# The 64x64 inverses of a delta-rule stage: products of both halves on two quarters of the tensor engine instead of one product with a diagonal left operand

## The chip, the cores and the metric

The kernel runs on one core of one Trainium2 chip. The metric is the time of one execution on the device, in microseconds: before the change 4966.08 us as the median of three runs (4948.15 to 4974.35). A core has five engines that matter here: TensorE (PE in the profile; its weight loads are PEld), VectorE (DVE), ScalarE (ACT), GpSimd (POOL) and SyncE (SP), which issues the DMAs.

## The reference, cut to what matters

The reference is a network of two blocks. Block 1 (a chunked mLSTM with dilated attention and a feed-forward part, two layers) and the attention, the merge and the experts of block 2 are not touched. The change lies in the second branch of block 2, a delta rule over 256 context tokens and then 512 tokens, in both directions, for 16 heads of 64 channels:

```python
def wkv_scan(s0, scan_in):
    def step(s, inp):
        w, kk, a, k, v, r = inp
        sa = jnp.einsum('dbhij,dbhj->dbhi', s, kk)
        s = s * w[..., None, :] - sa[..., :, None] * (kk * a)[..., None, :] + v[..., :, None] * k[..., None, :]
        return s, jnp.einsum('dbhij,dbhj->dbhi', s, r)
    return lax.scan(step, s0, scan_in)
```

A token's `sa` depends on all tokens before it. The kernel takes chunks of 64 tokens; within a chunk the dependence is a triangular system, so each chunk of each head and direction needs the inverse of a 64x64 triangular matrix.

## The kernel before

`rwkv` (L1499) works through eight blocks of 128 channels (two heads). A block has three groups of four chunks (four of context, then four and four of the 512 tokens), so there are 24 groups. The loop over `s` at the end of `rwkv` makes one pass for each group, and `weave` puts the steps of several generators side by side over `TT` = 36 ticks: `chain` of group s (the state over its four chunks), `newton` of group s + 1 once for each direction, `values` of group s + 1, `decays` and `products` of group s + 2, and as filler the projections of the next block (`mm` tiles in the profile, weights `wbh`, `wbl`). TensorE's instructions keep the order in which they are written (`pe = Pinned(...)`); the order on VectorE, ScalarE and GpSimd is set by the scheduler and by priorities (`high_priority`).

`newton` (L1723) takes the products G of a group, makes NB, and lays it out in fp16: N16 (L1733, ScalarE) and the rest NL (L1737, GpSimd). NB holds eight units of 64x64, four in partitions 0 to 63 and four in 64 to 127. Then `inverse` (L1957) runs 18 steps: `turned` is a transpose by 64x64 products with the unit matrix (two of it in each call), `prod` is one or two 64x64 products for each unit (15 of the steps), and each step ends in an evacuation to fp16 by ScalarE (`act`, L1986, tiles Yi and Zi) or VectorE (`plus`, L2000, tiles Ai and the first Yi). The last step adds into U (`keep`, L1745), which `chain` takes.

`prod` makes one instruction of 128x128 shape for two units, one in either half: its left operand (the stationary one) is a tile with the two units in diagonal blocks and zeros around them, its right operand has them stacked. So what is to stand on the left is copied into such a tile by `lay` (L1994, VectorE), half by half: Ly, Lv and Lz for each direction. N16 and NL are laid out in this way when they are made. All these tiles are cleared once by GpSimd (L1926).

Names in the rows: `n` is the PSUM bank of a step; `n<-Zi,Lv` is a product with moving operand Zi and left operand Lv; `c` the bank of the chain (`Xs`, `S`, `VS`, `KB`, `G`, `U`, `KR` its operands), `x` a bank of decays, products and transposes, `mm` one of the projections; `N` is N16 or N8; `id` and `tables` are unit matrices and masks.

Of the kernel before, what the change touches and what calls it, by code (L numbers as in the profile page):

```python
# [12 lines left out]
F16 = mybir.dt.float16  # L13
# [3 lines left out]
ALU = mybir.AluOpType  # L17
# [13 lines left out]
HL = 50  # L31
# [23 lines left out]
class Pinned:  # L55
    """An engine with its instructions in the order they are written in."""
# [9 lines left out]
class Core:  # L66
    """All engines so."""
# [7 lines left out]
class Feed:  # L75
    """Weights in the order of their use, 512 columns a tile, loaded ahead and split into two parts that one pass each carries."""

    def __init__(self, net, raw, split):
        self.net, self.nraw, self.nsplit = net, raw, split
        self.src, self.raws, self.tiles, self.over = [], [], {}, set()  # L80
        self.taken = self.dead = 0
        # another pool for what is loaded before weight number last
        self.more, self.last = None, 0

    def add(self, w, r0, c0, n, order=None, both=False):
        """1024 rows of n columns; returns the number of row tiles in a tile."""
        kt = min(KD, T // n)
        for rows in order or [range(k, k + kt) for k in range(0, KD, kt)]:
            self.src.append((w, r0 + rows[0] * P, rows[1] - rows[0], kt, c0, n, both))
        return kt  # L90
# [39 lines left out]
def part(gen, n):  # L130
    """The next n steps of a generator."""
# [11 lines left out]
def among(a, b, n):  # L143
    """A generator with n steps of another one after each of its own."""
# [5 lines left out]
def weave(ticks, *work):  # L150
    """Steps of several generators in turn: (generator or (function, its argument), from, to, number of steps)."""
# [12 lines left out]
def tables():  # L164
    """Constants of shapes alone, [128, n] each: for all of the program, for block 1, for block 2."""
# [20 lines left out]
    # axial rotation, token major: [128, token tile, 64]  # L186
# [23 lines left out]
class Net:  # L210
# [34 lines left out]
    def row(self, ap, n, pool=None, tag=None):  # L245
        """A DRAM row of n on all partitions."""
# [4 lines left out]
    def wtile(self, w, r0, c0, n):  # L251
        """128 rows of a weight, split into two parts that one pass each carries."""
# [16 lines left out]
    def rstd(self, out, ss, n, eps=1e-6, nc=None):  # L269
        """out = (ss / n + eps) ** -0.5"""  # L270
# [12 lines left out]
    def defer(self, n, f, *x):  # L283
        """f, n steps of the projections later."""
# [12 lines left out]
    def unit_t(self, w, c0, x, evac, n=P, tok=slice(0, T)):  # L297
        """Eight steps to a block of columns of a product, transposed: evac(psum [n, tokens])."""
# [19 lines left out]
    def unit_n(self, w, r0, c0, x, evac, pairs=(0, 1), order=((0, 1), (2, 3), (4, 5), (6, 7))):  # L318
        """Eight steps to 256 columns of a product of each pair of token tiles: evac(pair, psum [tokens, 2, 256])."""
# [23 lines left out]
    def norm_pair(self, p, g, x, pool, s=1):  # L343
        """Two token tiles of X, normed, to columns of the transposed operand: staged, s steps for each stage."""
# [36 lines left out]
    def layer(self, l, S):  # L381
        """The layers of block 1 in two parts: the order of what meets the weights; the work. The heads run on a plan of
        ticks, 24 for a head of the first kind (M) and 12 for one of the second (B), and projections are woven in."""
# [13 lines left out]
        # ---- what follows the projections  # L397
# [49 lines left out]
        def rope(nm, b):  # L447
            """Rotated queries or keys of two heads, split as the products of scores take them."""
# [57 lines left out]
        # ---- the order of the weights  # L506
# [34 lines left out]
        # ---- the heads  # L541
# [5 lines left out]
        def pofs(d, i, t):  # L547
            """Column of key tile i, query tile t among the kept blocks."""
# [89 lines left out]
        def turned(n, src, k):  # L638
            """128 columns of a mixed output, transposed and split."""
# [67 lines left out]
        # ---- the work  # L707
# [69 lines left out]
    def norms(self, name, g, S):  # L777
        """What the staged norm of the two pairs of token tiles takes, and a new transposed operand."""
# [5 lines left out]
    def block1(self):  # L784
        tc, nc, a = self.tc, self.nc, self.a
        with ExitStack() as st:
            # on the way into block 2: the transposed operand, and until then X
# [8 lines left out]
            # the table of functions, before data is there  # L796
# [30 lines left out]
    def final_part(self, p, s, k):  # L827
        """X times the final gain, 256 columns of a pair of token tiles, and their sums of squares before and after."""
# [11 lines left out]
    def final_rest(self, p, xs, mod, bank, x, s, n0):  # L840
        """X = rms_norm(X, final_g) of two token tiles; normed once more, scaled and shifted per feature, to columns of
        the transposed operand. Staged, s steps for each stage."""
# [52 lines left out]
    def gates(self, l, ps, q, tl):  # L895
        """The gates of block 1 from their sums: staged."""
# [85 lines left out]
    def ahead(self, S):  # L982
        """What block 2 takes from its conditions and its context alone."""
# [16 lines left out]
    def block2_params(self, pool):  # L1000
# [16 lines left out]
        # lambda, the same on all partitions  # L1017
# [11 lines left out]
    def attn_params(self, cp):  # L1029
        nc, a = self.nc, self.a  # L1030
        self.load_tables(2, cp)
        # gains of q and k folded into the rotation
# [24 lines left out]
    def mods(self, pool):  # L1057
        """Modulation vectors: per feature columns, and rows for the two that gate a residual."""
# [48 lines left out]
    def modulated_xt(self, tiles, s1, sh, xh, xl, pool, bank, back=None, first=0, to=None):  # L1107
        """Normalised token tiles -> split transposed operand, scaled and shifted per feature, or as it is to DRAM."""
# [21 lines left out]
    def normed_of(self, src, pool, out=None):  # L1130
        """src / rms, in a tile of the pool or over src."""
# [10 lines left out]
    def block2(self):  # L1142
# [17 lines left out]
        # the operands of the projections again as places for others: of [128, T], high and low  # L1160
# [26 lines left out]
    def attention(self):  # L1187
        """Differential attention, a quarter (two heads) at a time; while the heads of one quarter run, the
        projections of the next are woven in. Yields once before x is needed, with the function that gives
        banks, and once before the last quarter, whose fill it is sent."""  # L1190
# [5 lines left out]
        with ExitStack() as left:  # L1196
# [8 lines left out]
            def loads():  # L1205
                """256 columns of the weight at a time, split in two: four tiles of two row tiles each."""
# [26 lines left out]
            def bank_of(i, xh, xl, b, evac, last=False):  # L1233
                """Projection i of two token tiles to 256 columns."""
# [14 lines left out]
            def headed(nm, q, o, rotate, last):  # L1249
                """Queries or keys of two token tiles: normed by heads, rotated, and split as the products take them."""  # L1250
# [52 lines left out]
            def ahead(u):  # L1303
                """What a quarter takes from the context: keys and values."""
# [37 lines left out]
            def scores(n):  # L1342
                """Products of queries and keys, and their exponentials: 4 ticks for each of a unit's four maps."""
# [28 lines left out]
            def turned(u):  # L1372
                """A quarter's outputs, transposed."""
# [16 lines left out]
            def outs(n, x):  # L1390
                """The difference of a unit's maps, transposed, and its product with the values."""
# [91 lines left out]
    def wblock(self):  # L1483
        """The next two row tiles of a block of 128 columns, of weights laid [128, block, 8, 128], split in two; others are asked for ahead."""
# [14 lines left out]
    def rwkv(self, hxh, hxl, hch, hcl, mmt2, bank2, lead):  # L1499
        """Delta-rule heads by chunks of 64 tokens, a block of 128 channels (two heads) at a time, both  # L1500
        directions together and in three groups: 4 chunks of context, then 4 and 4 of x. While the chain
        over the chunks of one group runs, the inverses of the next, the decays of the one after it and
        the projections of the next block are woven in."""
# [7 lines left out]
        with ExitStack() as st:  # L1511
# [12 lines left out]
            # what no chain takes: gives way to the work that fills the last ones  # L1524
# [21 lines left out]
            def proj(b, dst, both=True):  # L1546
                """Shifted channels of block b, of context and x."""
# [1114 lines left out]
```

## Time and profile before

| what | us |
|---|---|
| median of three runs | 4966.08 |
| lowest, highest | 4948.15, 4974.35 |
| profiled execution, first to last instruction (span) | 4986.3 |
| TensorE busy in the span | 4530.2 |
| VectorE busy | 3463.8 |
| GpSimd busy | 2156.0 |
| ScalarE busy | 1993.8 |
| the stage with the 24 groups, 2030 to 3200 | 1170 |

Of the profiled execution the span is what is given; no other time of it is. Busy time of TensorE counts a product from its start to a modelled end, and products overlap: one that starts 0.03 us after another is still booked with its full 0.19 us. How fast a row of products goes is therefore read from start to start. The profile also gives the clock that TensorE was granted, as a share of full speed; it has two levels, 2.4 GHz (1.00) and 1.2 GHz (0.50).

### The profile page before, as it was taken

Reading aid. Unit: us, or ns where it says so; the run is one execution under the profiler, and the core shown is the slowest. Engines: PE = TensorE matmul, PEld = TensorE weight load, DVE = VectorE, ACT = ScalarE, POOL = GpSimd, SP = SyncE. Lnnn points to the kernel's source line nnn. Section 1 sums busy time; section 2 is a strip of 40 time slices with the busy share of each in tenths; the row PEclk is TensorE's granted clock in tenths of the full one; section 3 lists DMA queues with packets and bytes.
Section 4 is the critical chain, followed back from the end, with each engine's and each line's share of the span. In section 5 each row is a group of like instructions: output and inputs, shape, how many; then the busy total and the mean of one; then the engine's idle time right before and its main releaser. Section 6 shows DMA issues by size and latency. Waiting matters only on the chain. (4 is left out here: it accounts for less than half of the span.)

```text
span 4986.3 us, 78323 instructions
## 1 busy us (share of the span) xinstructions
PE 4530.2 (91%) x29167; PEld 3864.4 (78%) x29167; DVE 3463.8 (69%) x6705; ACT 1993.8 (40%) x4288; POOL 2156.0 (43%) x1715
## 2 busy tenths in 40 slices
PE   8999999999998998888898889889799889988987
PEld 6789897888888886677776767768677678877776
DVE  4654234655656654677777877668753989999999
ACT  3444334443325554344444444433222444333333
POOL 3324443324434332322232333144433247888886
PEclk8999999999999999788788888999678999999999
DMA  4234333235653211000000001462344447887886
GB/s 128 72 86 133 96 115 98 69 89 157 189 186 112 55 46 42 19 21 18 20 21 23 23 26 36 134 213 92 104 125 153 158 160 274 294 289 278 289 291 230
DMA packets 435687, 618.46 MB, mean 124 GB/s; under 512 B 32596, under 2 KB 318436, under 8 KB 435176
## 3 DMA queue, kind: packets, MB, share of 16 engines
q1 hardware_dynamic: 392104, 469.87, 30.0%
q0 software_dynamic: 36864, 134.23, 7.8%
q10 hardware_dynamic: 6336, 9.35, 0.6%
q8 instruction: 229, 3.75, 0.3%
q14 instruction: 154, 1.26, 0.1%
HBM read 549.36 MB, written 48.24 MB: 120 GB/s over the span
## 5 line engine op out<-in xcount | busy, mean ns | idle before, releaser
L63 POOL TENSOR_TENSOR wlo<-wraw,whi 128x512 fp32r<-128x512 f32 x451 | 614.9, 1369 | 897.3 <-ACT whi L63 850.6
L63 ACT CAST whi<-wraw 128x512 fp32r<-128x512 f32 x572 | 347.3, 617 | 564.4 <-PE mm L63 369.8
L63 PE MATMUL acc<-v,ah 128*128 128x512 f32 x1536 | 444.7, 414 | 4.3 <-ACT ah L63 4.3
L1495 POOL TENSOR_TENSOR wbl<-wblk,wbh 128x256 fp32r<-128x256 f32 (+1 forms) x184 | 148.3, 806 | 615.4 <-ACT wbh L1494 362.9
L63 PE MATMUL u<-hph,u 128*128 128x384 f32 x1504 | 400.6, 338 | 4.5 <-ACT x L63 4.5
L63 PE MATMUL mm<-whi,u 128*128 128x256 f32 x2048 | 377.2, 285 | 4.5 <-ACT u L63 2.7
L63 PE MATMUL acc<-v,al 128*128 128x512 f32 x768 | 264.2, 427 | 113.1 <-DVE al L63 112.8
L63 PEld LDWEIGHTS acc<-v,ah 128*128 128x128 f32 x1536 | 309.0, 202 | 68.0 <-ACT ah L63 4.6
L63 PE MATMUL mm<-xh,whi 128*128 128x512 f32 (+2 forms) x880 | 342.8, 390 | 8.0 <-ACT r L63 4.6
L63 PE MATMUL mm<-xh,wlo 128*128 128x512 f32 (+2 forms) x880 | 328.9, 374 | 0.0
L63 PEld LDWEIGHTS mm<-whi,u 128*128 128x128 f32 x2048 | 323.4, 193 | 6.5 <-ACT u L63 3.3
L63 PE MATMUL mm<-xl,whi 128*128 128x512 f32 (+2 forms) x880 | 328.4, 373 | 0.0
L63 POOL TENSOR_TENSOR u<-raw,u 128x1024 fp32r<-128x1024 f32 x94 | 273.3, 2908 | 81.0 <-ACT u L63 80.8
L63 ACT ACTIVATE gq<-gq 128x384 f32<-128x384 f32 x128 | 67.1, 524 | 595.4 <-DVE gq L63 595.4
L63 PE MATMUL mm<-wlo,u 128*128 128x256 f32 x1024 | 291.6, 285 | 5.0 <-POOL wlo L63 4.6
L63 PEld LDWEIGHTS acc<-v,al 128*128 128x128 f32 x768 | 151.5, 205 | 169.4 <-DVE al L63 140.4
L63 PEld LDWEIGHTS u<-hph,u 128*128 128x128 f32 x1504 | 275.4, 189 | 9.1 <-ACT x L63 4.9
L63 DVE SCALAR_TENSOR_TENSOR x<-gq,x 128x384 f32<-128x384 f32 x128 | 264.6, 2067 | 12.9 <-ACT gq L63 12.2
L63 POOL TENSOR_TENSOR v<-raw,v 128x1024 fp32r<-128x1024 f32 x64 | 195.1, 3048 | 171.7 <-ACT v L63 159.6
L63 PE MATMUL u<-hpl,u 128*128 128x384 f32 x752 | 253.5, 337 | 0.0
L63 PE MATMUL mm<-whi,xh 128*128 128x256 f32 x768 | 236.0, 307 | 0.0
L63 PE MATMUL mm<-whi,xl 128*128 128x256 f32 x768 | 219.5, 286 | 0.1
(608 smaller groups left out, 13232.8 us busy)
## 6 DMA issues: line engine op xcount, KB each, us to landing
raw<-in_ut_dram SPq DMA_DIRECT2D x128, 512.0 KB
raw<-in_peer_v_dram SPq DMA_DIRECT2D x128, 512.0 KB
wraw<-in_w_in_dram SPq DMA_DIRECT2D x184, 256.0 KB
wraw<-in_w_down_dram SPq DMA_DIRECT2D x160, 256.0 KB
wraw<-in_w_up_dram SPq DMA_DIRECT2D x152, 256.0 KB
mraw<-in_w_mod_dram SPq DMA_DIRECT2D x96, 256.0 KB
wg<-stage SPq DMA_DIRECT2D x12, 2048.0 KB
W<-wg SPq DMA_DIRECT2D x32, 768.0 KB
```

Of the source, the lines that this page charges most:

```text
L63: return lambda *a, **k: self.tc.keep_in_program_order(f(*a, **k))
L1495: (nc.vector if self.wn > WN and n % 2 else nc.gpsimd).tensor_tensor(lo, raw, hi.bitcast(F32), op=ALU.subtract)
```

## The change

The left operands are no longer laid out in diagonal blocks. `prod` makes two products of 64x64 shape for each pair of units instead of one of 128x128: the upper half of the partitions with the upper half of the result, the lower with the lower, each with its stacked operand as it was evacuated. With that `lay` and its copies go, the tiles Ly, Lv and Lz go, N16 and NL are stacked like NB and are each made by one instruction instead of two, and only U is cleared. The steps, their order and their evacuations stay. (The diff also drops comments and doc strings throughout the file, which moves line numbers by one to fourteen.)

```diff
-                for hf in H:
-                    nc.scalar.copy(N16[hf, u, hf], NB[hf])
+                nc.scalar.copy(N16[:, u], NB)
...
-                for hf in H:
-                    nc.gpsimd.tensor_tensor(NL[hf, u, hf], NB[hf], N16[hf, u, hf], op=ALU.subtract)
+                nc.gpsimd.tensor_tensor(NL[:, u], NB, N16[:, u], op=ALU.subtract)
...
-            N16, NL = (rest[0].tile([P, 8, P], F16, name=nm) for nm in ("N16", "NL"))
-            L_ = [[rest[0].tile([P, 4, P], F16, name=f"L{nm}{d}") for nm in "yvz"] for d in range(2)]
+            N16, NL = (rest[0].tile([P, 8, 64], F16, name=nm) for nm in ("N16", "NL"))
             U_ = rest[0].tile([P, 4, 2, P], F32, name="U")
-            for x in (N16, NL, *L_[0], *L_[1], U_):
-                nc.gpsimd.memset(x, 0.0)
+            nc.gpsimd.memset(U_, 0.0)
...
                 for n, (l, r) in enumerate(pairs):
-                    pe.matmul(ps[:, i * 64:(i + 1) * 64], l[:, i], r[:, i], start=n == 0, stop=n == len(pairs) - 1)
+                    for hf in H:
+                        pe.matmul(ps[hf, i * 64:(i + 1) * 64], l[hf, i], r[hf, i], start=n == 0, stop=n == len(pairs) - 1)
...
-        def act(ps, tag, left=None):
+        def act(ps, tag):
             t = t16(tag)
             with self.tc.high_priority(HP):
                 nc.scalar.copy(t, ps)
-            lay(left, t)
             return t
 
-        def lay(left, t):
-            if left is not None:
-                with self.tc.high_priority(HL):
-                    for hf in H:
-                        nc.vector.tensor_copy(left[hf, :, hf], t[hf])
...
-        Y = plus(turned(N8), 2.0, "Yi", Ly)
+        Y = plus(turned(N8), 2.0, "Yi")
         yield
-        plus(prod((Ly, N8)), 2.0, "Ai", Lv)
+        V = plus(prod((Y, N8)), 2.0, "Ai")
         yield
-        Y = act(prod((Lv, Y)), "Yi", Ly)
+        Y = act(prod((V, Y)), "Yi")
...
         for it in range(3):
-            A = plus(prod((N16, Y)), 2.0, "Ai", Lv if it < 2 else None)
+            A = plus(prod((N16, Y)), 2.0, "Ai")
             yield
-            Y = act(prod((Lz, A)), "Yi")
+            Y = act(prod((Z, A)), "Yi")
             yield
-            Z = act(prod((Lv, Z)), "Zi", Lz) if it < 2 else act(turned(Y), "Zi")
+            Z = act(prod((A, Z)) if it < 2 else turned(Y), "Zi")
             yield
-        plus(prod((N16, Y), (NL, Y)), 1.0, "Ai", Lv)
+        A = plus(prod((N16, Y), (NL, Y)), 1.0, "Ai")
         yield
-        keep(prod((Lv, Z)), Z)
+        keep(prod((A, Z)), Z)
```

How the change moves instructions is seen at two places. The first is TensorE early in the stage, at the third step of an inverse (Y = V Y); before, the left operand of the first direction is Lv_20448 and that of the second Lv_20451:

```order
L63 MATMUL mm_20489<-xl_15441,wbh_20522 128x512
L63 LDWEIGHTS Lv_20448
L63 MATMUL n_3909_20685<-Yi_3898_20633,Lv_20448 128x64
...
L63 LDWEIGHTS Lv_20451
L63 MATMUL n_3911_20694<-Yi_3900_20646,Lv_20451 128x64
...
L63 MATMUL mm_20489<-xh_15440,wbl_20523 128x512
```

and in the changed kernel:

```order
L62 MATMUL mm_20475<-xl_15441,wbh_20508 128x512
L62 LDWEIGHTS Ai_3903_20646
L62 MATMUL n_3909_20667<-Yi_3898_20615,Ai_3903_20646 64x64
...
L62 LDWEIGHTS Ai_3905_20657
L62 MATMUL n_3911_20678<-Yi_3900_20626,Ai_3905_20657 64x64
...
L62 MATMUL mm_20475<-xh_15440,wbl_20509 128x512
```

The left operand is now the evacuated tile itself, and each direction has eight pairs of load and product where it had four; the projections around them stay where they were, as do all other products of TensorE.

The second place is VectorE at the first two steps of an inverse in a later group, before:

```order
L1792 COPY VS_21628<-c_20443 64x128
L2000 SCALAR_TENSOR_TENSOR Yi_4147_21788<-tables_19359,n_4146_21779 128x256
L2000 SCALAR_TENSOR_TENSOR Yi_4149_21801<-tables_19359,n_4148_21792 128x256
L1994 COPY Ly_20447<-Yi_4147_21788 64x4x64 x2
L1994 COPY Ly_20450<-Yi_4149_21801 64x4x64 x2
L1804 SCALAR_TENSOR_TENSOR S_21818<-c_20443,WC_20594,Sw_21729 128x128 x2
L2000 SCALAR_TENSOR_TENSOR Ai_4153_21826<-tables_19359,n_4152_21821 128x256
L2000 SCALAR_TENSOR_TENSOR Ai_4155_21835<-tables_19359,n_4154_21830 128x256
L1994 COPY Lv_20448<-Ai_4153_21826 64x4x64 x2
L1994 COPY Lv_20451<-Ai_4155_21835 64x4x64 x2
L1671 SCALAR_TENSOR_TENSOR ta_21734<-ta_21734,kkn_20795 128x256
L1775 COPY Xs_21851<-c_20443 64x128
```

and in the changed kernel:

```order
L1987 SCALAR_TENSOR_TENSOR Yi_4147_21938<-tables_19359,n_4146_21929 128x256
L1789 COPY VS_21762<-c_20443 64x128
L1987 SCALAR_TENSOR_TENSOR Yi_4149_21949<-tables_19359,n_4148_21940 128x256
L1801 SCALAR_TENSOR_TENSOR S_21964<-c_20443,WC_20580,Sw_21883 128x128 x2
L1987 SCALAR_TENSOR_TENSOR Ai_4153_21976<-tables_19359,n_4152_21967 128x256
L1987 SCALAR_TENSOR_TENSOR Ai_4155_21987<-tables_19359,n_4154_21978 128x256
L1670 SCALAR_TENSOR_TENSOR ta_21888<-ta_21888,kkn_20797 128x256 x2
L1772 COPY Xs_22001<-c_20443 64x128
```

The copies into Ly and Lv are gone; the rest moves by a place or two.

## Rows read from the trace of the kernel before

**Rows 1.** The page: TensorE's granted clock in 40 slices of the span, tenths.
```profile
PEclk8999999999999999788788888999678999999999
```

**Rows 2.** Stage: length, busy PE, PEld, DVE, ACT, POOL (instructions), granted clock, DMA share, GB/s.
```profile
2030.00:3200.00 1170.00, 1026.14 (x9313) 824.09 (x9311) 894.74 (x2523) 506.68 (x1420) 343.29 (x517) 0.83 0.10 31
```

**Rows 3.** Groups of instructions, 2030 to 3200: busy us, mean ns | idle before, releasers.
```profile
L1994 DVE COPY Lv<-Ai 64x256 f16<-64x256 f16 x480 | 165.1, 344 | 6.8
...
L1994 DVE COPY Lz<-Zi 64x256 f16<-64x256 f16 x288 | 71.4, 248 | 10.9 <-ACT Zi L1986 6.1
L63 PE MATMUL c<-Xs,U 128*128 128x64 f32 x368 | 64.9, 309 | 28.0 <-DVE Y L1782 22.2 <-ACT Y L1780 3.3 <-DVE U L1745 1.1
...
L1994 DVE COPY Ly<-Yi 64x256 f16<-64x256 f16 x192 | 63.8, 332 | 3.0
...
L63 PE MATMUL n<-Zi,Lv 128*128 128x64 f16 x576 | 36.1, 203 | 47.3 <-DVE Lv L1994 47.3
...
L63 PE MATMUL n<-N,Ly 128*128 128x64 f16 x384 | 30.3, 222 | 20.4 <-DVE Ly L1994 19.2 <-ACT wbh L1494 0.4
...
L63 PE MATMUL n<-Yi,Lv 128*128 128x64 f16 x384 | 24.9, 209 | 14.2 <-DVE Lv L1994 14.0 <-ACT Zi L1986 0.2
```

**Rows 4.** Who waited for whom, 2030 to 3200: us in total, times, longest.
```profile
PE n L63 <- DVE Lv L1994: 61.3, 61, 2.0
...
PE n L63 <- DVE Ly L1994: 19.2, 34, 1.8
```

**Rows 5.** One wait in order of time: start us, us, engine, instruction, [idle before].
```profile
2407.86 0.74 DVE L2000 SCALAR_TENSOR_TENSOR Ai<-tables,n 128x256 f16<-128x256 f32 x2
...
2408.52 1.79 DVE L1994 COPY Lv<-Ai 64x256 f16<-64x256 f16 x4
...
2409.40 0.29 PE L63 MATMUL n<-Zi,Lv 128*128 128x64 f16 x4 [1.73 <-DVE Lv L1994]
...
2410.37 0.39 PE L63 MATMUL n<-Zi,Lv 128*128 128x64 f16 x4 [0.68 <-DVE Lv L1994]
```

**Rows 6.** Short stretches ahead of and behind falls of the clock, columns as in rows 2.
```profile
2406.50:2409.90 3.40, 1.46 (x11) 0.85 (x10) 3.32 (x7) 1.86 (x5) 3.17 (x5) 1.00 0.14 41
2409.90:2430.40 20.50, 20.03 (x113) 17.76 (x113) 9.37 (x28) 6.02 (x16) 4.53 (x5) 0.50 0.03 7
2034.40:2037.80 3.40, 1.41 (x16) 0.79 (x16) 3.26 (x9) 1.77 (x5) 2.10 (x3) 1.00 0.14 41
...
3140.30:3143.70 3.40, 1.49 (x13) 1.02 (x13) 3.28 (x7) 1.11 (x3) 2.80 (x5) 1.00 0.14 41
...
2181.20:2184.60 3.40, 0.94 (x7) 0.49 (x5) 3.10 (x9) 1.00 (x2) 1.31 (x2) 1.00 0.12 32
```

**Rows 7.** TensorE alone in order of time, at 1.00: large products, then transposes.
```profile
2398.34 0.47 PE L63 MATMUL mm<-xl,wbh 128*128 128x512 f32 x1
2398.66 0.41 PE L63 MATMUL n<-Zi,Lv 128*128 128x64 f16 x8
2398.90 0.48 PE L63 MATMUL mm<-xh,wbl 128*128 128x512 f32 x1
...
2400.26 0.41 PE L63 MATMUL n<-Yi,N 128*128 128x64 f16 x8
2400.60 1.16 PE L63 MATMUL x<-KR,BK 64*128 64x128 f32 x8
...
2402.27 0.40 PE L63 MATMUL mm<-xl,wbh 128*128 128x512 f32 x1
2402.50 0.41 PE L63 MATMUL n<-Ai,Lz 128*128 128x64 f16 x8
...
2404.24 0.51 PE L63 MATMUL mm<-xh,wbh 128*128 128x512 f32 x1
2404.68 0.44 PE L63 MATMUL n<-id,Yi 64*64 64x64 f16 x16
2405.05 0.50 PE L63 MATMUL mm<-xl,wbh 128*128 128x512 f32 x1
```

More of the change, by code (lines that the diff above doesn't have):

```diff
@@ L30 @@
 HP = 1000
-HL = 50
 HC = 1000
@@ L1748, in newton @@
                 yield from self.inverse(N16[:, u], NL[:, u], N8, eye, id16, lambda: bank(f"n{d}", 1),
-                                    lambda sh, tag, b, dt: tl(sh, f"{tag}{d}", b, dt), L_[d], keep, pe)
+                                    lambda sh, tag, b, dt: tl(sh, f"{tag}{d}", b, dt), keep, pe)
             def chain(o, g):
@@ L1955, in rwkv, with inverse @@
             weave(30, (self.rwkv_post(os_[-1], tl, xt, SG, pp, pe), 0, 30, 4), (fill, 0, 30, NE[2]))
-    def inverse(self, N16, NL, N8, eye, id16, nwt, tl, L, keep, pe):
+    def inverse(self, N16, NL, N8, eye, id16, nwt, tl, keep, pe):
         nc = self.nc
@@ L1962, in inverse @@
         H = (slice(0, 64), slice(64, 128))
-        Ly, Lv, Lz = L
         t16 = lambda tag: tl([P, nk, 64], tag, 2, F16)
@@ L1986, in act, with plus @@
                 nc.scalar.copy(t, ps)
-            lay(left, t)
             return t
-        def lay(left, t):
-            if left is not None:
-                with self.tc.high_priority(HL):
-                    for hf in H:
-                        nc.vector.tensor_copy(left[hf, :, hf], t[hf])
-        def plus(ps, f, tag, left=None):
+        def plus(ps, f, tag):
             t = t16(tag)
@@ L2000, in plus @@
                 nc.vector.scalar_tensor_tensor(t, unit, f, ps, op0=ALU.mult, op1=ALU.add)
-            lay(left, t)
             return t
-        Y = plus(turned(N8), 2.0, "Yi", Ly)
+        Y = plus(turned(N8), 2.0, "Yi")
         yield
-        plus(prod((Ly, N8)), 2.0, "Ai", Lv)
+        V = plus(prod((Y, N8)), 2.0, "Ai")
         yield
-        Y = act(prod((Lv, Y)), "Yi", Ly)
+        Y = act(prod((V, Y)), "Yi")
         yield
-        V = plus(prod((Ly, N8)), 2.0, "Ai", Lv)
+        V = plus(prod((Y, N8)), 2.0, "Ai")
         yield
-        Z = act(prod((Ly, V)), "Zi", Lz)
+        Z = act(prod((Y, V)), "Zi")
         yield
-        Y = act(prod((Lv, Y)), "Yi")
+        Y = act(prod((V, Y)), "Yi")
         yield
         for it in range(3):
-            A = plus(prod((N16, Y)), 2.0, "Ai", Lv if it < 2 else None)
+            A = plus(prod((N16, Y)), 2.0, "Ai")
             yield
-            Y = act(prod((Lz, A)), "Yi")
+            Y = act(prod((Z, A)), "Yi")
             yield
-            Z = act(prod((Lv, Z)), "Zi", Lz) if it < 2 else act(turned(Y), "Zi")
+            Z = act(prod((A, Z)) if it < 2 else turned(Y), "Zi")
             yield
-        plus(prod((N16, Y), (NL, Y)), 1.0, "Ai", Lv)
+        A = plus(prod((N16, Y), (NL, Y)), 1.0, "Ai")
         yield
-        keep(prod((Lv, Z)), Z)
+        keep(prod((A, Z)), Z)
         yield
```

## The prediction

> **What bounds the kernel now.** I read the page first, and there the row of granted clocks. It shows where TensorE runs at full speed: eights and sevens in slices 17 to 25, nines elsewhere [rows 1]. The change lies in those slices only, so the second view is the stretch from 2030 to 3200 us by itself, the stage in which the 24 chunk groups run. There TensorE is booked for 1026.1 of 1170 us, VectorE for 894.7, ScalarE for 506.7 and GpSimd for 343.3, at a mean granted clock of 0.83 [rows 2]. TensorE takes its work in program order, so the stage lasts as long as its work plus the 144 us in which it waits, and its work lasts twice as long where the clock stands at 1.2 instead of 2.4 GHz. A mean of 0.83 says that (1 - 0.83) / 0.5 = 34% of the stage, 398 us, went by at the lower level.
>
> The third view says what TensorE waits for. Of its 144 us idle, products with a laid-out left operand (Lv, Ly) hold 47.3 + 20.4 + 14.2 = 82 us, and the state chain's product with U holds 28.0 [rows 3]. The waits by cause say the same: 61 waits, 61.3 us, for the copies into Lv and 34 waits, 19.2 us, for those into Ly [rows 4]. One such wait in order of time [rows 5]: both Ai are evacuated by 2407.86 + 0.74 = 2408.60, the four copies run from 2408.52 to 2410.31 (marks of merged rows overlap a little), and TensorE, free since 2409.40 - 1.73 = 2407.67, starts the first half-group at 2409.40 and the second at 2410.37. About 1.8 us lie between the operand's being there and its being laid out.
>
> The fourth view is the clock around such waits [rows 6]. From 2406.5 to 2409.9, which holds the wait of rows 5, the clock is still at 1.00 and TensorE is busy for 1.46 of 3.4 us; then 20.5 us run at 0.50. The stretches that begin at 2034.4 and 3140.3 look the same, and the one at 2181.2 is one of the chain's waits, 0.94 us busy. Going through the stage like this I count 31 falls; 18 of them, the first at 2037.8 and the last of these at 3143.7, stand behind waits for Lv, Ly or Lz.
>
> **The change part by part.** *Copies removed.* 480 + 288 + 192 = 960 copies, 165.1 + 71.4 + 63.8 = 300 us of VectorE's 895, a third [rows 3]. None is on TensorE's path by its duration, only by the waits behind it. Of 15 product steps seven take a left operand that was made just before, and there the copy is the last thing that TensorE waits for. The 95 waits of rows 4 are 80.5 us. Beside that, a group that need not wait starts about 0.15 us before the modelled end of its predecessor (2398.66 against 2398.34 + 0.47) [rows 7], which a waiting one loses too: 95 x 0.15 = 14. What stays: a left operand that was just made is not loaded ahead, so the group begins 0.32 instead of 0.23 us after its predecessor's start (2398.34 to 2398.66, 2402.27 to 2402.50) [rows 7], some 95 x 0.1 = 9 us; and Ai itself can be late, as in rows 5, where TensorE would have waited until 2408.6 even without the copies; I put 5 us for all. **Gain 80.5 + 14 - 9 - 5 = 80 us**, at least 60.
>
> *Products on quarters.* 360 places of the TensorE order (24 groups x 15 steps, both directions side by side) go from 8 products of 128x128 shape to 16 of 64x64, and 24 of them from 16 to 32; nothing else of TensorE's order moves. The shape 64x64 is in the trace already: the transposes, n<-id. In time, 16 products of it take 0.44 us against 0.41 for 8 large ones [rows 7]. Less the 0.19 that a single one lasts, 15 steps make 0.25 and 7 steps make 0.22: the halves run beside each other, 16 ns apart, and the group itself costs 0.03 more. The change of shape costs more. Between two projections of 128x512 the transposes take 2404.24 to 2404.68 to 2405.05, 0.81 us from the start of the one before to the start of the one behind; the large products take 2398.34 to 2398.66 to 2398.90, 0.56. So a place costs 0.25 us: 0.1 ahead (0.44 against 0.32, said as 0.1), the rest behind. Where the neighbour has another shape already, the price is paid today: n<-Yi,N at 2400.26 is followed at 2400.60 by a 64x128 product, 0.34 us where 0.24 is enough ahead of a projection. I counted neighbours in the order: ahead of 298 places stands a product of 128x128 shape, ahead of 62 one of 128x64; behind 314 stands one of 128x128, behind 46 one of 64x128. For the 62 the trace has no 64x64 row; the bounds are 0 and 0.1, I take the middle. 298 x 0.1 + 62 x 0.05 + 314 x 0.125 + 46 x 0.03 = 30 + 3 + 39 + 1 = **a cost of 74 us**, 70 to 77 by these bounds.
>
> A rule speaks against this step. The Trainium skill, TensorEngine Tiling (Array Packing), "Instruction Overhead", says that each matmul has about 60 cycles of overhead, so that a narrow one is no cheaper; at 2.4 GHz that is an estimate of 25 ns, and 16 would take 0.40 us a place, 0.15 more than the row's 0.25, some 54 us in all. The transposes at 2404.68 do not show it, 16 ns apart; they go to two separate quarters, as the new products will.
>
> *VectorE with a third less to do.* The wait for U's product, 28.0 us, is put down mostly to L1782 on VectorE (22.2 us) [rows 3], which stands in the same queue as the copies. I take 8 us back, between 0 and 22.
>
> *The clock.* If the 18 falls go, 18/31 of 398 us = 231 us are worked at 2.4 instead of 1.2 GHz, which gives back half, 115 us. But a stretch that does not fall there may fall at the next wait of the chain, 13 of which stay, and the shape changes add short gaps. I take half: **a gain of 58 us**, between 0 and 115.
>
> *Edits at nothing.* N16 and NL in one piece instead of two shorten ScalarE and GpSimd, which are booked for 506.7 and 343.3 of 1170 us [rows 2] and which no long wait of TensorE's ends on [rows 3]. The eight clears of the diagonal tiles leave GpSimd at the stage's start, where TensorE does not wait for it either. The cover is ample.
>
> **Sum.** -80 + 74 - 8 - 58 = -72 us. Against the profiled execution's span of 4986.3 that is 4914; that span stands 0.4% above the median of the runs, 4966.08, so the time is 4966 - 72 = 4894, said as 4895. What a measurement of this kernel can tell from no change is about 0.5%, 25 us: faster means under 4941, slower over 4991.
>
> **The rivals.** *A wash.* Waits and shape changes cancel (-80 + 74), and the clock falls as often, now behind the chain's waits. For it: 13 falls stand behind other waits already, such as the chain's [rows 6]. Against it: a wait of the chain that comes while the clock is low makes no fall today, and there is less on VectorE to wait for. 4966 - 6 - 8 = 4952. Chance 0.18.
>
> *Slower: the changes of shape keep the clock down.* The place is the stage again: the array empties twice at each of 360 places, 0.25 us each, where before there were 95 waits, fewer but longer. If this holds TensorE at 1.2 GHz for half as long again, 398 becomes 600 us and costs 100: 4966 - 14 + 100 = 5052. It decides above the point where the lower level takes 398 + 2 x 39 = 476 us of the stage, at a mean granted clock near 0.80. Against it: of the 31 falls none stands behind changes of shape alone; each has waits ahead of it that add up to 0.7 us or more. Chance 0.09.
>
> *Slower: the halves do not overlap.* If 16 small products take twice the time of 8 large ones, each place costs 0.22 more, the 24 long ones 0.44, together 85 us: 4894 + 85 = 4979, and with the clock's gain half lost 5008. The transposes speak against it [rows 7]; what differs is that both operands are new. Chance 0.03. By the rule of the Trainium skill named above the loss would be its 54 us and the time 4949, which is the wash; it shares this chance.
>
> *That the change doesn't do what it says:* the order of VectorE in the changed kernel has no copy into Lv, Ly or Lz any more, so this is left out.
>
> **How the numbers follow.** The forecast has 0.70, the wash 0.18, the slower ones 0.12, and these are the chances of faster, within 0.5% and slower. The low end takes every gain at its bound: -80 + 70 - 22 - 115 = -147, near 4820; I stop at 4830. The high end has the waits' gain at 60, the full cost and no help from the clock, 4966 + 77 - 60 = 4983, said as 4985; it takes in the wash and leaves out the two slower rivals' worse half.
>
> **What would show it.** In the profile of the changed kernel: no L1994 rows, and VectorE near 600 us in the stage; a place between two projections near 0.8 us, with 16 ns between its products; TensorE's waits at n under 15 us; a mean granted clock of about 0.9; the stage shorter by some 70 us. The prediction is wrong if the clock stays at 0.83 or below, if a place costs clearly more or less than 0.25 us, or if the chain's waits grow by what the others lose.

## The result, and the profile after

| | before | after |
|---|---|---|
| time, median | 4969.55 us (4948.15 to 4974.35) | 4800.36 us (4792.93 to 4804.98) |
| profiled execution: span | 4986.3 us | 4791.0 us |
| stage of the 24 chunk groups | 2030 to 3200, 1170 us | 2030 to 3014, 984 us |

After takes 0.9661 of the time of before, 95% interval 0.963 to 0.9692: 169 us less. 186 of the 195 us between the two spans lie in the stage; what follows it lasts 1777 us where it lasted 1786. The direction was forecast, the size was not: 72 us were forecast, and 4800 lies under the range of 4830 to 4985.

The granted clock over the whole span, of after (to [rows 1]):

```profile
PEclk9999999999999999899999999998788999999999
```

The stage and what follows it, of after, columns as in [rows 2]:

```profile
2030.00:3014.00 984.00, 949.00 (x12384) 747.74 (x12384) 623.29 (x1561) 484.42 (x1372) 314.75 (x467) 0.96 0.13 37
3014.00:4791.00 1777.00, 1598.18 (x7438) 1348.71 (x7437) 1483.89 (x2258) 628.29 (x1062) 1030.11 (x561) 0.91 0.62 210
```

The dip of the clock in slices 17 to 25 is gone but for one eight. The one in slices 28 to 31 stays; it was there before too, in 29 to 31 [rows 1], where the prediction read nines. In the stage it is 0.96 where it was 0.83, so the lower level holds (1 - 0.96) / 0.5 x 984 = 79 us instead of 398; I count 7 falls where there were 31. TensorE is idle for 984 - 949 = 35 us (144 before), and although it issues a third more products its booked time fell by 77 us.

Not every fall stands behind a wait. Two of the 7 come at 2351.3 and 2603.9; from 2345 to the first TensorE idles for 0.25 us, from 2598 to the second not at all. Shortly ahead of both stand twelve products of two columns each, here those of the second:

```profile
2602.65 1.43 PE L62 MATMUL x<-tables,sq 128*128 128x2 f32 x12
```

Groups of instructions of after in the stage, columns as in [rows 3]:

```profile
L62 PE MATMUL c<-Xs,U 128*128 128x64 f32 x368 | 54.0, 270 | 7.5 <-DVE Y L1779 4.7 <-ACT Y L1777 2.8
...
L62 PE MATMUL n<-Zi,Ai 64*64 64x64 f16 x1152 | 33.0, 196 | 2.7 <-DVE Ai L1987 2.6
...
L1734 POOL TENSOR_TENSOR NL<-NB,N 128x256 f16<-128x256 f32 x47 | 31.2, 684 | 47.1 <-ACT N L1731 42.5 <-PE x L62 3.5 <-PE mm L62 1.0
...
L62 PE MATMUL n<-N,Yi 64*64 64x64 f16 x768 | 22.9, 204 | 0.0
...
L62 PE MATMUL n<-Yi,Ai 64*64 64x64 f16 x768 | 22.0, 199 | 0.0
```

What TensorE waited for in the stage of after (to [rows 4]; us in total, times, longest):

```profile
PE c L62 <- DVE S L1801: 7.4, 8, 1.3
PE c L62 <- DVE VS L1789: 5.5, 10, 1.0
PE x L62 <- DVE kkn L1598: 4.8, 3, 2.0
PE c L62 <- DVE Y L1779: 4.7, 10, 1.4
...
PE n L62 <- DVE Ai L1987: 3.2, 6, 0.6
```

The three groups that held 47.3, 20.4 and 14.2 us now hold 2.7, 0.0 and 0.0. But the product with U, which the change doesn't touch, fell from 28.0 to 7.5: that is more than the 8 us taken back for it, and the first sign of where the rest comes from.

TensorE alone in order of time, of after: a place between two projections, and one behind a 128x64 product (to [rows 7]):

```profile
2380.97 0.48 PE L62 MATMUL mm<-xl,wbh 128*128 128x512 f32 x1
2381.38 0.44 PE L62 MATMUL n<-Zi,Ai 64*64 64x64 f16 x16
2381.75 0.50 PE L62 MATMUL mm<-xh,wbl 128*128 128x512 f32 x1
...
2108.59 0.45 PE L62 MATMUL c<-VS,KB 128*64 128x64 f32 x8
2108.97 0.44 PE L62 MATMUL n<-N,Yi 64*64 64x64 f16 x16
```

From 2380.97 to 2381.75 are 0.78 us, where 0.81 was forecast and the large shape took 0.56. Over all places between two projections at a clock of 1.00 the medians of the traces are 0.33 us ahead and 0.37 behind in after (164 places), 0.24 and 0.24 in before (135), so a place costs 0.21 us. Sixteen products take 0.44 us, 16 ns apart on the average, as the transposes did. In truth they come in pairs: the two halves of a pair start 3 ns apart in the trace, and a pair follows the last after 31 ns, as one large product follows another. It can be seen where pairs of N and NL alternate, of after:

```profile
3010.24 0.20 PE L62 MATMUL n<-Yi,N 64*64 64x64 f16 x2
3010.27 0.20 PE L62 MATMUL n<-Yi,NL 64*64 64x64 f16 x2
```

Behind a 128x64 product the group starts 0.38 us after its predecessor, 2108.59 to 2108.97, as large ones did before (2392.05 to 2392.43 there): no price of entry.

### The profile page after: what moved, and what is told of

Same layout as the page of the kernel before. It is cut to its first block, busy times and chain, and to the rows that moved or that the text cites. A ratio compares the mean times of both kernels' runs of the same rounds, so it can differ in the third digit from the quotient of the medians.

```text
span 4791.0 us, 83411 instructions
## 1 busy us (share of the span) xinstructions
PE 4447.0 (93%) x32239; PEld 3784.4 (79%) x32239; DVE 3195.4 (67%) x5745; ACT 1971.2 (41%) x4240; POOL 2117.7 (44%) x1659
```

## The experiments

Times are medians, with the ratio to the kernel before on the same chip and its 95% interval. Differences between kernels are taken from the ratios, times 4970; each is good to about 15 us.

**Which part of the change does what.** The change removes the waits, changes the shape and unloads VectorE. Three kernels do these one at a time. *quarters_copies* is before with the new shape, its left operands still read from the diagonal blocks:

```diff
-                    pe.matmul(ps[:, i * 64:(i + 1) * 64], l[:, i], r[:, i], start=n == 0, stop=n == len(pairs) - 1)
+                    for hf in H:
+                        pe.matmul(ps[hf, i * 64:(i + 1) * 64], l[hf, i, hf], r[hf, i], start=n == 0, stop=n == len(pairs) - 1)
```

> The kernel before with one part of the change: products of 64x64 shape, but their left operands still come out of the diagonal tiles, so all 960 copies and the waits for them stay. Theory 1 (the gain came from the waits for the copies, directly and through the falls of the clock they cause; the shape itself costs about 0.2 us at each of 360 places): slower than before by about 70 us, 5035, or more if the clock falls oftener; mean granted clock of the stage 0.80 to 0.84, TensorE's waits at n about 80 us. Rival 2 (the quarter products themselves keep the clock up, since there are twice as many of them): faster than before, under 4920, with a granted clock above 0.9 in the stage although the waits are still there.

Measured: 5043.4 us, 1.0132 (1.0104 to 1.016), so +66. The clock stays at 0.83, so the small shape does not keep it up. The waits at n are shorter than expected, 59 us instead of 80 (quarters_copies, 2030 to 3255, with 1.5 us for Ai):

```profile
PE n L63 <- DVE Lv L1995: 47.3, 84, 1.5
...
PE n L63 <- DVE Ly L1995: 10.1, 23, 1.1
```

So the +66 is the price of the shape less what the waits lost. In the two stages TensorE is booked for 1121.4 instead of 1026.1 us and idle for 108 instead of 144.

*large_no_copies* is before without the copies, in the large shape:

```diff
-                    pe.matmul(ps[:, i * 64:(i + 1) * 64], l[:, i], r[:, i], start=n == 0, stop=n == len(pairs) - 1)
+                    pe.matmul(ps[:, i * 64:(i + 1) * 64], id16, r[:, i], start=n == 0, stop=n == len(pairs) - 1)
...
-            if left is not None:
+            if False:
```

> The other part of the change alone: products of 128x128 shape as before, but no copies. Left out: the left operand of every step is a constant unit matrix and the newest evacuated tile is the right operand, so each step still waits for the step before it, and the inverses are not computed. Theory 1: faster than the changed kernel by the price of the shape, about 70 us, so near 4730, with a granted clock in the stage of 0.96 or more and waits at n of a few us. Rival 2 (the quarters keep the clock up): the clock stays below 0.9 and the time above 4850.

Measured: 4753.2 us, 0.9554 (0.9529 to 0.9579). Its stage, columns as in [rows 2]:

```profile
2030.00:2968.00 938.00, 885.45 (x9311) 715.50 (x9310) 631.14 (x1564) 499.23 (x1420) 350.32 (x520) 0.96 0.13 38
```

The clock is 0.96 in the large shape too once the copies are gone, so the quarters are not what keeps it up. From this side the shape costs 53 us (0.9661 against 0.9554; 41 by a second measurement of after, below), somewhat less than the 70 expected; a left operand that never changes is no exact control.

*quarters_dead_copies* is after with the 960 copies back on VectorE, at their old priority, into tiles that nobody reads:

```diff
+            self.dead = [[rest[0].tile([P, 4, P], F16, name=f"L{nm}{d}") for nm in "yvz"] for d in range(2)]
...
+        def lay(left, t):
+            if left is not None:
+                with self.tc.high_priority(50):
+                    for hf in H:
+                        nc.vector.tensor_copy(left[hf, :, hf], t[hf])
...
```

> The changed kernel, with the 960 copies of before made all the same, into diagonal tiles that nobody reads: VectorE has its old load of about 895 us in the stage, but no product waits for a copy. Theory 1 (the wait for the copy was what cost): 4800 to 4830, granted clock of the stage above 0.93, waits of the chain's products somewhat longer. Rival 3 (VectorE's load as such made everything late, the chain's Xs, VS and S too): above 4880, clock below 0.9 and waits of the chain back at 28 us and more.

Measured: 4954.6 us, 0.9958 (0.9939 to 0.9977). The rival holds: copies that TensorE never waits for cost 148 us. The stages of quarters_copies and of quarters_dead_copies, columns as in [rows 2]:

```profile
2030.00:3259.00 1229.00, 1121.44 (x12396) 876.36 (x12395) 899.09 (x2527) 513.18 (x1422) 346.55 (x525) 0.83 0.10 30
```

```profile
2030.00:3182.00 1152.00, 1064.94 (x12369) 831.13 (x12368) 876.53 (x2520) 487.47 (x1370) 306.69 (x467) 0.85 0.10 32
```

Against after's row the second has the same products on TensorE, 52 us more idle time and 116 us more booked time. That is the clock: at 0.85 the lower level holds 346 us, at 0.96 it held 79, and half of the difference is 133. The waits of the same stage say behind what:

```profile
PE c L62 <- DVE Y L1779: 22.3, 12, 3.6
PE x L62 <- DVE kkn L1598: 14.2, 5, 4.0
PE c L62 <- DVE VS L1789: 13.5, 12, 1.8
PE n L62 <- DVE Ai L1995: 7.8, 10, 1.8
```

One of them in order of time, of the same kernel, and the clock ahead of its end and behind it:

```profile
2593.50 0.46 DVE L1989 COPY Lv<-Ai 64x256 f16<-64x256 f16 x2
2593.97 0.46 DVE L1989 COPY Ly<-Yi 64x256 f16<-64x256 f16 x2
...
2595.34 0.47 PE L62 MATMUL mm<-xl,wbh 128*128 128x512 f32 x1
2595.44 0.45 DVE L1989 COPY Ly<-Yi 64x256 f16<-64x256 f16 x2
...
2595.91 1.81 DVE L1989 COPY Lv<-Ai 64x256 f16<-64x256 f16 x4
...
2597.73 0.58 DVE L1779 TENSOR_TENSOR Y<-Y,c 64x128 f32<-64x128 f32 x2
...
2598.37 1.10 PE L62 MATMUL c<-Xs,U 128*128 128x64 f32 x4 [2.55 <-DVE Y L1779]
```

```profile
2595.00:2598.40 3.40, 0.85 (x8) 0.54 (x6) 3.31 (x13) 1.15 (x3) 1.33 (x3) 1.00 0.14 41
2598.40:2605.20 6.80, 6.80 (x54) 4.83 (x54) 5.01 (x16) 2.54 (x8) 0.90 (x3) 0.50 0.03 7
```

VectorE is not idle between the first of these copies and Y. The product with U needs the bank that Y reads; Y's input has been ready since TensorE's last product into c, before 2593, but ten of the dead copies, 3.18 us, stand ahead of Y in VectorE's queue, the last six of them directly. TensorE waits 2.55 us, and from 2598.4 the clock stands at 1.2 GHz.

*quarters_half_dead* keeps only the 480 copies of Y and Z (against quarters_dead_copies; the other copies of Ai go the same way):

```diff
-        V = plus(prod((Y, N8)), 2.0, "Ai", Lv)
+        V = plus(prod((Y, N8)), 2.0, "Ai")
...
```

> The changed kernel with half of the copies that nobody reads: those into the tiles for Y and Z (480, about 150 us of VectorE), none into that for A. Theory 3 as the first runs left it (what the copies cost is VectorE's load, through later evacuations of the chain and of the steps): about half of the 155 us that all of them cost, 4860 to 4890. Rival 6 (only the copies right behind an evacuation that is waited for, those of A, do harm): 4800 to 4825.

Measured: 4857.1 us, 0.9749 (0.9727 to 0.9771): 44 us for the copies of Y and Z and 104 for those of Ai. That is 3 us under the range of the load theory and 32 us above that of rival 6. The copies of Ai last longer (341 ns in quarters_dead_copies, with 303 and 249 for the others) and are 164 of the 294 us of copies, 56%, but 70% of the price: load alone does not set it.

**Queue order, load, or copies held up.** *quarters_dead_late* has the same dead copies with `high_priority(-400)` in place of 50, so that the scheduler puts them behind wanted work.

> The same 960 copies that nobody reads as in quarters_dead_copies, with the same work for VectorE, but at a low priority: in VectorE's order they stand some places later, behind evacuations that something waits for. Theory 3a (a copy costs because a wanted evacuation stands behind it in the queue): clearly less than the 155 us of the copies in their old places, 4830 to 4900, granted clock 0.89 or more. Rival 8 (it is the sum of VectorE's work, or what the copies do to the memory, wherever they stand): within 15 us of 4955, clock 0.85.

Measured: 4882.6 us, 0.984 (0.981 to 0.9869). Its stage, and the costliest of TensorE's waits in it:

```profile
2030.00:3097.00 1067.00, 997.16 (x12393) 782.30 (x12393) 869.25 (x2524) 486.64 (x1372) 310.66 (x467) 0.92 0.12 34
...
PE c L62 <- DVE S L1799: 19.9, 7, 3.9
```

VectorE is booked for as much in the stage (869 us against 877), but 59 of the 148 us are gone (72 of 154 by the medians): that much was the place in the queue. Y's wait falls from 22.3 to 4.2 us; another comes up, 19.9 us for S in seven waits. One of these shows copies of 0.22 us lasting up to 1.35 (quarters_dead_late in order of time):

```profile
2348.84 1.04 POOL L2046 TENSOR_TENSOR Y<-Y,r 128x512 f32<-128x512 f32 x1
...
2348.96 5.04 DVE L1989 COPY Ly<-Yi 64x256 f16<-64x256 f16 x4
...
2349.96 1.28 POOL L2047 TENSOR_TENSOR Y<-Y,parp 128x512 f32<-128x512 f32 x1
...
2351.32 1.26 POOL L2048 TENSOR_TENSOR Y<-Y,parp 128x512 f32<-128x512 f32 x1
...
2352.66 1.26 POOL L2052 TENSOR_TENSOR Y<-Y,post 128x512 f32<-128x512 f32 x1
...
2354.03 0.61 DVE L1799 TENSOR_SCALAR S<-c,WC 128x128 f32<-128x128 f32 x2
...
2354.70 0.45 PE L62 MATMUL c<-S,KR 128*64 128x128 f32 x2 [3.75 <-DVE S L1799]
```

The four copies end about 0.08 us behind GpSimd's four instructions, one behind each, and late as they are they still stand ahead of S, for which TensorE waits 3.75 us. This leaves one more rival: not the load, but copies held up by GpSimd. *quarters_dead_reduce* and *quarters_dead_reduce_late* put a reduction of about the same booked time in each copy's place (against quarters_dead_copies; the tiles are made to fit):

```diff
-                        nc.vector.tensor_copy(left[hf, :, hf], t[hf])
+                        nc.vector.tensor_reduce(out=left[hf], in_=t[hf, :, :40].rearrange("p a (b c) -> p a b c", c=2), op=ALU.max, axis=AX.X)
```

> The changed kernel with 960 useless instructions on VectorE at the places of the copies, as in quarters_dead_copies, but each a reduction of 64x160 f16 instead of a copy of 64x256 f16. A copy there lasts 0.224 us at the median and up to 1.36; the long ones end together with an instruction of GpSimd. Worked out from the reductions of the trace of before (128x512 in 676 ns, 128x768 in 956 ns) one of 64x160 should last 0.29 us, 280 us for all, as much as the copies (293). Theory: it is VectorE's load and its order alone: 4800 + 155 x 280 / 293 = 4948 us. Rival 9: it is the copies that GpSimd holds up, and a reduction is not held: under 4900 us, the longest of them near the median.

> The same reductions issued late, as the copies in quarters_dead_late (4883 us). Theory (load and order alone): as there, 4883 us. Rival 9 (what remained of the price there is copies that GpSimd holds up, such as four in 5.04 us ahead of a state that TensorE waited 3.75 us for): under 4840 us, and the wait for the state under 8 us where it was 19.9.

Measured: 4954.0 us, 0.9953 (0.9936 to 0.997), and 4890.9 us, 0.9819 (0.9802 to 0.9836). One tile's instructions, ns at least, median and most, of quarters_dead_late and of quarters_dead_reduce_late:

```profile
L1989 DVE COPY Ly<-Yi x192: 208/224/1352, 2036.6 to 3059.6; 64x256 f16<-64x256 f16 x192
```

```profile
L1989 DVE TENSOR_REDUCE Ly<-Yi x192: 299/313/318, 2030.8 to 3073.6; 64x80 f32<-64x160 f16 x192
```

No reduction is held up, each lasts 0.30 to 0.32 us, and the price is the same within the 15 us, early and late. The wait for S does go, as the rival said, from 19.9 to 0.9 us, but another takes its place; quarters_dead_reduce_late, 2030 to 3175:

```profile
PE n L62 <- DVE Ai L1995: 19.7, 18, 4.2
```

In quarters_dead_late this one was 7.7 us. The rival falls: being held up is real, but what costs is VectorE's load and where it stands in the queue.

**Does the clock pay?** *before_filler* adds 672 useless 128x128 products of 256 columns to before, two ahead of each step whose left operand was just copied:

```diff
+            for m in range(2):
+                pe.matmul(ps[:, 256:], self.fl[:, m, :P], self.fl[:, m, :256], start=True, stop=True)
```

> The kernel before with useless work added: ahead of each direction's products at the seven steps that take a just-made left operand, two more 128x128 products of 256 columns go into the unused half of the step's bank (672 in all, about 0.12 us each at 2.4 GHz: 81 us of TensorE). Theory 4 (what a wait costs is mostly the fall of the clock behind it, and work in its place keeps the clock up): the waits at n fall from 82 to under 30 us, the granted clock of the stage rises to 0.87 or more, and the time is the same or lower than before, 4900 to 4975, in spite of the added work. Rival 5 (the clock in the stage is low for other reasons and a wait costs its own length only): at best the added work is hidden in the waits, else it is added; 4985 to 5050, clock 0.83.

Measured: 4977.6 us, 1.0014 (0.9992 to 1.0037). The stage of before_filler, and its new group:

```profile
2030.00:3186.00 1156.00, 1061.16 (x9954) 867.81 (x9955) 894.97 (x2521) 511.06 (x1415) 342.21 (x512) 0.90 0.10 31
...
L63 PE MATMUL n<-xh 128*128 128x256 f32 x672 | 168.1, 339 | 9.7 <-ACT xh L1872 6.1 <-DVE Ai L2007 3.2 <-ACT Zi L1993 0.2
```

The waits at n fell only from 82 to 41 us, not under 30, and the time is 3 us over the expected range; but the added work costs nothing that can be measured: the clock rises from 0.83 to 0.90 (lower level 231 instead of 398 us), and TensorE idles for 95 instead of 144 us.

*after_filler* has the same filler in after, where it has no waits to fill.

> The same useless products added to the changed kernel, where no waits at n are left to fill; they also part the two directions, which makes two more changes of shape at each of 168 places. Both theories: their price in full, 81 us and some 168 x 0.22 = 37 us, 4800 + 118 = 4918, with the clock at 0.95 or more. This is the price that the kernel before with the same filler is to be read against.

Measured: 4934.9 us, 0.9899 (0.9881 to 0.9917): 118 to 135 us, by the ratio and by the medians. The clock was expected at 0.95 or more and is lower than in after; its stage:

```profile
2030.00:3174.00 1144.00, 1116.41 (x12994) 883.00 (x12993) 627.14 (x1555) 494.83 (x1365) 309.15 (x464) 0.93 0.11 32
```

What is free in before is paid in full in after. The two prices are not quite the same thing: in after the filler adds changes of shape, 37 of the 118 us by the estimate above, which before doesn't have; and why the clock is lower stays open.

**Can it be made better?** *quarters_n_large* is after with N16 and NL in diagonal blocks again, so that the four steps whose left operand is known long before keep the large shape.

> The changed kernel, but N16 and NL are laid out in diagonal blocks when they are made, as before, and the four steps of an inverse that have them on the left use products of 128x128 shape. No copies come back. 96 of the 360 places keep the projections' shape. Theory 1 with a price of 0.22 us a place, 0.28 at the 24 long ones: 4800 - 23 = 4777. If the time stays within 5 us of 4800, the price of a shape is hidden by other waits; if it is higher, the two pieces of ScalarE and GpSimd work instead of one have become waits.

Measured: 4807.9 us, 0.9664 (0.9642 to 0.9685), the same as after; the 23 us that were expected did not come. TensorE is booked for 9 us less, and its wait for S is 14.7 us where after has 7.4.

Three kernels move more of VectorE's work in after to GpSimd: *quarters_light* a product of BK and the copy into VS,

> The changed kernel with less on VectorE still: one of the two products that make BK (46 of 482 ns) and the copy of the values into VS (44 of 336 ns) go to GpSimd, 36 us of VectorE's 623 in the stage. Theory 3, in proportion (300 us of load cost 155): faster by up to 19 us, 4780. Rival 7 (below some load VectorE is no longer late and nothing is gained): 4800, or a few us more if GpSimd's products take longer than VectorE's and the chain waits for them.

*quarters_light2* the copies into WC and VS,

> The changed kernel with two kinds of small copies moved from VectorE to GpSimd that are made a group or two before they are used: the values into VS (44 of 336 ns) and the last decays WC (46 of 390 ns), 33 us of VectorE. Unlike in quarters_light, no product moves. If the loss of quarters_light came from BK's product on GpSimd being late, this one is at 4800 or up to 17 us below; if it came from VectorE's order being another (rival 7), it is again above 4810.

and *quarters_light3* those two copies in quarters_n_large.

> quarters_n_large and quarters_light2 together: the four steps with N16 and NL on the left in 128x128 shape, and the two small copies on GpSimd. If the price of the shapes (23 us for these places) was covered in quarters_n_large by waits for VectorE's update of S, and these small copies stand in its way, 4760 to 4785; if the waits for S stay, 4800 to 4815.

Measured: 4824.0 us, 0.9688 (0.9669 to 0.9707); 4783.1 us, 0.963 (0.9611 to 0.9648); 4787.3 us, 0.9632 (0.9615 to 0.9649), just outside what was expected of it. The first missed both of its values: TensorE's wait for S grows to 18.6 us. Since the copies of quarters_light2 do no harm, it is put down to the product of BK; in what way stays open. *after_again* is after once more, for the comparison with quarters_light2.

> The changed kernel itself once more, beside the kernel before on the same chip as other runs, to read quarters_light2 (ratio 0.963, 0.9611 to 0.9648) against: the same ratio as in the first measurement, 0.966. If its interval lies above 0.9648, quarters_light2 is the faster of the two.

Measured: 4799.1 us, 0.9636 (0.9613 to 0.9658). This is 12 us under the first measurement by the ratio, and quarters_light2 can't be told from it. None of these four kernels beats after by more than the measurement is uncertain.

## Why the prediction was right in direction and wrong in size

The change taken step by step, by the ratios: shape +66 us (before to quarters_copies), products no longer waiting for copies -87 (to quarters_dead_copies, where N16 and NL are in one piece as well), copies off VectorE -148 (to after); together -169. In the prediction's own terms, read from the stages of the two traces: waits at n -79 (forecast -80 with what goes with them), other waits of TensorE -30 (forecast -8), the lower level of the clock -160 (forecast -58), and the shape the rest of the 186 us, +83 (forecast +74).

- **Where the time lies, and the waits at n:** right. The stage holds 186 of 195 us; the waits went from 82 to 3 us.
- **Products on quarters, +74:** right in size: +83 by that account, of which +66 are left in the time with the copies kept and 41 to 53 without, because other waits get shorter. The 62 places behind a 128x64 product cost nothing rather than the 0.05 us in the sum. The rival *halves do not overlap* falls with the 3 ns between the halves of a pair. What the prediction made of the Trainium skill, TensorEngine Tiling (Array Packing), "Instruction Overhead", falls too: with 60 cycles a product, an estimated 25 ns, added up over both quarters, 16 would start over 0.38 us; the row shows 0.44 us in all, of which one product is 0.19, so 15 steps make 0.25. Taken for each quarter by itself the page's figure is not contradicted: there the products start 31 ns apart.
- **"VectorE with a third less to do", -8, at most 22:** this step failed. The prediction saw that Y, which ends the wait for U's product, stands in the same queue as the copies, but it took that one wait of 22 us for all that the load could cost. "None is on TensorE's path by its duration, only by the waits behind it" is what quarters_dead_copies refutes: the copies cost 148 us there without one of TensorE's products reading them. In the wait that is shown ten of them stand ahead of Y, which TensorE does wait for; behind such waits the clock falls, and that is most of the price (in the traces 116 us of booked time, 52 idle). Of the 148 us 59 went when the copies were put later (quarters_dead_late); in the one wait of the rest that is shown, four of them still stand ahead of S. The load and the place in the queue are not split further.
- **The clock, -58, bounded at 115:** this failed with it, and it is the larger number. The prediction tied the gain to the 18 falls behind waits for copies and let the 13 behind other waits stand. Once the copies were off VectorE those other waits shortened too, and 7 falls were left: (398 - 79) / 2 = 160 us given back (149 by the trace of after_again, 0.95 over 1005 us). These did not come with the waits at n: with the copies still on VectorE 27 falls remain, at 0.85, and only (398 - 346) / 2 = 26 us are given back.
- **Rivals.** The wash said that the clock would fall as often, now behind the chain's waits, at 4952. That is close to what happens when the copies stay on VectorE: 27 falls and 4954.6. *The changes of shape keep the clock down* is wrong: 0.83 with the new shape and the copies, 0.96 without them.
- **Edits at nothing:** nothing speaks against it, but no run has them alone. NL takes 47 x 684 ns where two halves took 96 x 672 (quarters_copies), and in after GpSimd ends no wait of TensorE's and ScalarE one above 1.6 us, for wbh (3.7), as before (3.6).

What stays open: the 89 us that late copies still cost (82 by the medians) are seen as waits for S or Ai and the falls behind them, but not split between them; and how the BK product harms quarters_light.

## What to carry to other kernels

An instruction that nobody waits for is not free on an in-order engine: look at what stands in that queue ahead of each evacuation that another engine does wait for, and count the engine's load there, not only the releaser's name. Where the clock falls behind waits, price a wait together with the fall: from quarters_dead_copies to after 52 us of idle time took 168 us of the stage with them, 3.2 for each. Fillers paid only where there were such waits: 672 useless products were free in before and cost at least 118 us in after, changes of shape included.

## What the hardware showed beside that

A change of product shape costs some 0.1 us ahead and as much behind (0.33 against 0.24 us, 0.37 against 0.24), but nothing ahead where the neighbour there is a 128x64 product (0.38 us before and after). Products of 64x64 on two quarters start 3 ns apart, while on one quarter they follow each other 31 ns apart, as large ones do. Copies of f16 within SBUF, 0.22 us at the median, lasted up to 1.36 us beside GpSimd's elementwise work and ended with its instructions, while reductions of 0.31 us at the same places never did; the Trainium skill, SBUF — State Buffer, "Who interferes with whom", says that the second of two such instructions is blocked by a shared pair of ports until the first ends, and the trace agrees. On GpSimd 128 partitions took as long as 64 (684 against 672 ns).
